# Four blocks of the first merge gate move from the stream to the opening, and the adaLN columns are turned by the identity

## The chip, the cores and the metric

The kernel runs on one core of a Trainium2 chip. The metric is device time in microseconds (us); the median of three runs before the change is 2131.4 us (2131.13 to 2132.64). The engines are named as the profile names them: PE is TensorE (PEld its weight loads), DVE is VectorE, ACT is ScalarE, POOL is GpSimd, SP is SyncE, which issues most DMAs.

## The reference

One layer of a decoder step with two parallel branches. The inputs are 256 prompt tokens and 8 samples of 8 tokens, so 320 token columns in all; the model width is 2048.

```python
mod = silu(c) @ w_ada + b_ada                       # 9 conditionings, 3 x 2048 features
shift, scale, gate = split(mod, 3)
h = rms_norm(x, pre_norm_g) * (1 + scale) + shift
(a_qkv, a_z, a_b, a_a, b_q, b_k, b_v, b_z, i_q, i_k, i_w, g_a, g_b) = split(h @ w_in)
y_a = gdn_branch(a_qkv, a_z, a_b, a_a, ...)         # gated delta rule, chunked
y_b = attend(b_q, b_k, b_v, i_q, i_w, i_k) * silu(b_z)
merged = sigmoid(g_a) * (y_a @ w_pa) + sigmoid(g_b) * (y_b @ w_pb)
out = rms_norm(merged @ w_out, post_norm_g)
return x + gate * out, ...
```

`attend` picks the top keys with an indexer (`i_q`, `i_k`, `i_w`) and attends to them only; for the samples the keys and values lie in a paged cache and are gathered. `g_a`, the input of the first merge gate, is 2048 features of `w_in`: 16 blocks of 128. Everything is float32 in and out.

## The kernel before, in words

**Products.** A block is 128 output features by 320 token columns, summed over 16 blocks of 128 input features. The weights are split into a high part (`whi`, a copy by ACT into the type that PE multiplies in one pass) and the remainder (`wlo`, a subtraction by DVE); the tokens `h` are split the same way into `xh` and `xl`. Each block of weights is used in three matmuls: `xh` by `whi`, `xl` by `whi`, `xh` by `wlo`. A block of the input projection is thus 16 x 3 = 48 matmuls.

**The opening** (`startup`, L493). The tokens `h` are not there at first: they need the conditioning `mod`, a product of `cT` (the nine conditionings, padded to 32 columns, stationary) with `w_ada`. The opening works in eight visits, q = 0 to 7. Visit q has these pieces:

- `columns`: the product of `cT` with the features of visit q, 256 of the shift and 256 of the scale, from four 1 MB loads. Four column groups of PE work side by side, each on every fourth block of input features, so that a bank of PSUM holds four partial sums in its four groups of 32 rows. ACT copies the bank to `msb`.
- `operands(q - 1)`, "the turn": six transposes of the tokens, then four float32 matmuls of `msb` with `sel`, which add the four partial sums and turn the features to the rows; DVE then makes `mod`, `gs`, `hT` and `xl`, ACT makes `xh`, for the two blocks of tokens of visit q - 1.
- `split_i(q - 1)` and `split(q - 1)`: high and low halves of the weights of the index queries (`whi`, `wlo`) and of a group of small projections (`awh`, `awl`; one buffer each).
- jobs, which queue in a first-in first-out list (`fifo`) and are taken by `run(n)`: per visit eight `iq_job` (index queries; 6 matmuls of 256 columns into a bank of PSUM, which two additions of DVE, into `q` and `qiS`, empty), one `bv_job`, and five `held_job` (6 matmuls of 320 columns each, into banks kept for the whole opening).

Three banks of PSUM go round among columns, turns and jobs. Each engine works its instructions off in the order in which this code writes them.

**The stream** (`stream`, L382) then takes one half block after the other (24 matmuls), from a list of chunks made in `attn_chunks` (the other index queries, queries, z, first gate, some more z) and `gdn_chunks`. Between them, generators ("sides") are stepped: the attention of the prompt, the eight samples (`sample_branch` and its successor), the gate of `mod` (`gate_gen`, which has columns and `sel` of its own kind), the delta rule. A planner decides when a side goes on, with a table of its own of how long instructions last. The first chunk of the delta rule may begin only when no side is left (`chunks[0].ready = lambda: not self.sides`, L1634): what the sides still have to do is then written out at once, with nothing of the stream in between.

One sample of the attention is, on PE, `esel` (the mask), `a,qS` (scores), 33 small `ident,a` (transposes of the probabilities), `a,a` and `vS,a` (products with the values), and one `ident,a` of 128 columns (the output); between these DVE takes maxima, ACT exponentials, DVE transposes the keys of the next sample (STREAM_TRANSPOSE), and POOL gathers keys and values.

Of the kernel before, what the change touches and what calls it, by code (L numbers as in the profile page):

```python
# [35 lines left out]
EARLY = 8  # L36
AHEAD = 4
# [167 lines left out]
class Kernel:  # L205
# [259 lines left out]
    def consts(self):  # L465
# [6 lines left out]
        self.ident_b = self.l0.tile([128, 128], BF, name="ident_b")  # L472
        v.tensor_copy(self.ident_b, self.ident)
# [19 lines left out]
    def startup(self):  # L493
# [12 lines left out]
        awl = sp.tile([128, 2, 720], F32R, name="awl")  # L506
        seq = []
        for q in range(8):
            seq += [("a", q, 0), ("a", q, 1), ("a", 8 + q, 0), ("a", 8 + q, 1), ("i", q, 0), ("w", q, 0)]
        raws, aws, iqs = {}, {}, {}  # L510
        pos = {"n": 0}

        def load():
            while pos["n"] < len(seq):
                kind, q, h = seq[pos["n"]]
                r = awr if kind == "w" else ring
# [8 lines left out]
                elif kind == "w":  # L525
                    for d0, c0, n in ((0, C_IK, 144), (144, C_BA, 64), (208, C_BK, 512)):
                        nc.sync.dma_start(t[:, :, d0:d0 + n], w[rows, c0:c0 + n].rearrange("(k p) c -> p k c", p=128))
                    aws[q] = t
                else:
# [15 lines left out]
        for e in range(2):  # L545
            nc.scalar.dma_start(x[2][64 * e:64 * e + 64], xs[:, 1024 * e:1024 * e + 1024])
# [21 lines left out]
        seli = sp.tile([128, 9, 4], I32, name="seli")  # L568
        nc.gpsimd.iota(seli, pattern=[[-1, 9], [-32, 4]], base=0, channel_multiplier=1)
        self4 = sp.tile([128, 9, 4], F32, name="self4")  # L570
        nc.vector.tensor_scalar(self4, seli, 0.0, None, op0=OP.is_equal)
        self.sel = self.l0.tile([128, 9], F32, name="sel")
        nc.vector.tensor_reduce(self.sel, self4, axis=AX.X, op=OP.add)
# [17 lines left out]
        both = sp.tile([128, 128], F32, name="both")  # L591
        for e in range(2):
            self.tt(both[:, 64 * e:64 * e + 64], self.ident[:, 0:64], self.ident[:, 64:128], OP.add)
# [23 lines left out]
        msb = sp.tile([128, 512], F32, name="msb")  # L617
# [14 lines left out]
        def split_i(q, g):  # L632
# [13 lines left out]
            low()  # L646

# [48 lines left out]

        def first_jobs():
# [8 lines left out]
        def jobs(q):  # L706
# [12 lines left out]
        def columns(q, e, h, p):  # L719
            t, whole = raws.pop((q + 8 * e, h))  # L720
            for k in range(8):
                kb, j = 8 * h + k, k % 4
                self.mm(p[32 * j:32 * j + 32, 256 * e:256 * e + 256], self.cT[:, kb, :], t[:, k, :], start=(kb < 4),
                        stop=(kb >= 12), skip=True)
            drop(t, whole)

        def operands(q, turned=None):
# [3 lines left out]
            for e in range(4):  # L731
                self.mm(p[:, 9 * e:9 * e + 9], msb[:, 128 * e:128 * e + 128], self.sel)
# [3 lines left out]
            for e, qq in enumerate((q, 8 + q)):  # L736
                self.tt(mod[:, 2 * qq:2 * qq + 2, :], p[:, 18 * e:18 * e + 18].rearrange("p (e s) -> p e s", s=9),
# [11 lines left out]
        for q in range(8):  # L749
# [12 lines left out]
            else:  # L762
                idle_turns(10)
# [6 lines left out]
            if q == 0:  # L770
                idle_turns(14)
            columns(q, 0, 1, p)
            if q == 0:
                idle_turns(14)
            elif q == 1:
                run(4)
            else:
                split(q - 1)
                run(5)
            if q >= AHEAD:  # L780
                split_i(q, 0)
            columns(q, 1, 0, p)
            if q == 0:
# [5 lines left out]
                idle_turns(8)  # L789
            columns(q, 1, 1, p)  # L790
            self.act(msb, p)
# [4 lines left out]
            elif q > 1:  # L796
                run(4)
# [10 lines left out]
        jobs(7)  # L808
        run(5)
        split(7)  # L810
        run(4)
        self.split_ahead(1)
        run(3)
        self.split_ahead(2)
        run(2)
# [12 lines left out]
    def gate_gen(self):  # L828
# [13 lines left out]
        for q in range(8):  # L842
# [6 lines left out]
            for k in range(KB):  # L849
                j = k % 4  # L850
                self.mm(p[32 * j:32 * j + 32, 0:256], self.cT[:, k, :], pend[k // 8][:, 256 * (k % 8):256 * (k % 8) + 256],
                        start=(k < 4), stop=(k >= 12), skip=True)
# [7 lines left out]
            self.act(m[:, 0:256], p[:, 0:256])  # L860
# [4 lines left out]
            for e in range(2):  # L865
                self.mm(p[:, 9 * e:9 * e + 9], m[:, 128 * e:128 * e + 128], self.sel)
            for e in range(2):
                k = 2 * q + e
                self.ts(self.gatp[:, k, :], p[:, 9 * e:9 * e + 9], self.feat[:, 32 + k:33 + k], self.feat[:, 64 + k:65 + k],
                        OP.add, OP.mult)  # L870
# [40 lines left out]
    def modulate(self, k, p, gs, mod, h):  # L911
        self.ts(h[:, :NP], p[:, :NP], gs[:, k, 0:1], mod[:, k, 0:1], OP.mult, OP.add)
        hs = h[:, NP:NT].rearrange("p (b t) -> p b t", t=TS)
        c0 = NP + 64 * (k // 8)
        bc = lambda a: a[:, k, 1:9].rearrange("p (b o) -> p b o", o=1).to_broadcast([128, NB, TS])
        self.tt(hs, p[:, c0:c0 + 64].rearrange("p (b t) -> p b t", t=TS), bc(gs), OP.mult)
# [86 lines left out]
    def attn_chunks(self):  # L1003
# [5 lines left out]
        ga = self.pairs(w, C_GA, 16, lambda p, h: self.gate_done(p, h, self.d_siga, self.t_r), r)  # L1009
# [1437 lines left out]
```

## Time and profile before

| | |
|---|---|
| median of three runs | 2131.4 us (2131.13 to 2132.64) |
| profiled execution, its own time | 2132.65 us |
| its span in the profile | 2130.9 us |
| PE busy | 2099.3 us, 99% |
| DVE, ACT, POOL busy | 1410.9, 989.6, 463.1 us |
| bytes moved by DMA | 438.91 MB, 206 GB/s on the mean |
| granted PE clock, mean | 0.998 |

The span is one execution as the profiler saw it; the times are those of executions without it. Busy time is an average over stages with different limits, so the stages are read one at a time: the opening lasts to about 170 us, the samples lie between 560 and 720 us. In a timeline a row gives start and length in us, engine, line, operation and tiles, how many instructions it holds, and in brackets the idle time before it with what ended it.

### The profile page before, as it was taken

The page shows a single profiled execution, that of the slowest core. Times are in us where ns is not written, and L with a number is a line of the kernel's source. Part 1 is how long each engine was busy: PE and PEld are TensorE (multiplying, and loading weights), DVE is VectorE, ACT ScalarE, POOL GpSimd, SP SyncE. Part 2 cuts the span into 40 slices and gives each one's busy share as a digit, 9 for nine tenths or more (in the row PEclk, how much of TensorE's full clock was granted, in tenths as well). Part 3 has the DMA queues.
Part 4 walks back from the last instruction along what each step waited for, and adds up shares of the span by engine and source line. Part 5 has one row for each costly group of instructions (what it writes and reads, how often), then busy time and mean ns, then how long its engine had stood idle before and what let it go on. Part 6 is the DMA issues. An engine that isn't in the chain of part 4 may idle for free.

```text
span 2130.9 us, 43963 instructions
## 1 busy us (share of the span) xinstructions
PE 2099.3 (99%) x17055; PEld 2006.3 (94%) x17055; DVE 1410.9 (66%) x2881; ACT 989.6 (46%) x2257; POOL 463.1 (22%) x653
## 2 busy tenths in 40 slices
PE   7999999999999999999999999999999999999997
PEld 5889999899999999999999999999999999999997
DVE  4665657899755678868787878787746545445543
ACT  3235464333344455565656565656535424233343
POOL 2000100000001036545444444445440000000000
PEclk9999999999999999999999999999999999999999
DMA  9996656985787766777877777777787967555562
GB/s 332 355 309 173 181 151 178 289 256 151 201 238 239 205 181 173 211 210 207 207 200 199 208 196 210 193 212 192 200 218 210 268 180 218 161 155 146 166 178 85
DMA packets 720336, 438.91 MB, mean 206 GB/s; under 512 B 74144, under 2 KB 705536, under 8 KB 717824
## 3 DMA queue, kind: packets, MB, share of 16 engines
q1 hardware_dynamic: 716032, 413.45, 68.9%
q0 software_dynamic: 3616, 21.02, 3.0%
q8 instruction: 134, 2.20, 0.4%
q10 hardware_dynamic: 480, 1.65, 0.3%
q14 instruction: 74, 0.61, 0.1%
HBM read 386.81 MB, written 48.94 MB: 204 GB/s over the span
## 4 chain that ended last, share of the span: by engine, by line
PE 72%; issue 23%; DMA 2%; DVE 2%; ACT 0%; SPq 0%; DVEq 0%; POOL 0%; POOLq 0%; ACTq 0%
PE pm L63 56%; PE ps L63 16%; DMA raw<-in_w_ada_dram 1%; DVE S L63 1%; DMA rawx<-in_w_in_dram 1%; DVE wlo L63 0%; SPq L63 0%; DMA c<-in_c_sample_dram 0%; DVE awl L63 0%; DMA out_dram<-S 0%; ACT whi L63 0%; ACT ot L63 0%; DVE sga L63 0%; DVE w L63 0%; DVEq L2443 0%
## 5 line engine op out<-in xcount | busy, mean ns | idle before, releaser
L63 PE MATMUL pm<-xh,whi 128*128 128x320 f32 (+1 forms) x3284 | 996.1, 317 | 1.9 <-DVE qiS L63 0.8
L63 PE MATMUL pm<-xl,whi 128*128 128x320 f32 (+1 forms) x3284 | 962.1, 307 | 0.4 <-DVE xl L63 0.3
L63 DVE TENSOR_TENSOR wlo<-raw,whi 128x1024 fp32r<-128x1024 f32 x474 | 589.1, 1252 | 280.8 <-ACT whi L63 264.9
L63 PEld LDWEIGHTS pm<-xh,whi 128*128 128x128 f32 x3284 | 617.6, 188 | 32.2 <-issue 23.9
L63 PEld LDWEIGHTS pm<-xl,whi 128*128 128x128 f32 x3284 | 618.1, 188 | 1.7 <-DVE xl L63 0.8
L63 ACT ACTIVATE whi<-raw 128x1024 fp32r<-128x1024 f32 x474 | 497.7, 1058 | 169.7 <-PE pm L63 150.8
L63 PE MATMUL pm<-xh,wlo 128*128 128x320 f32 (+1 forms) x3284 | 547.6, 307 | 0.0
L63 PEld LDWEIGHTS pm<-xh,wlo 128*128 128x128 f32 x3284 | 495.4, 188 | 0.0
L63 POOL TENSOR_TENSOR X<-X,tmpx 48x31 f32<-48x31 f32 (+15 forms) x248 | 175.9, 709 | 19.4
L63 POOL TENSOR_TENSOR tmpx<-blk,X 48x31 f32<-48x31 f32 (+15 forms) x248 | 160.4, 647 | 51.0 <-DMA blk<-d_b 32.8
L63 PE MATMUL pm<-y1h,whi 128*128 128x320 f32 x512 | 151.3, 308 | 1.1 <-ACT y1h L63 1.1
L63 PE MATMUL pm<-y1l,whi 128*128 128x320 f32 x512 | 151.3, 307 | 0.2
L63 DVE SCALAR_TENSOR_TENSOR ps<-xp,cs,ps 128x344 f32<-128x344 f32 x192 | 111.5, 581 | 6.8
L63 POOL TENSOR_TENSOR rfin<-rfin,mh 128x3 f32<-128x3 f32 x1 | 0.8, 848 | 486.4 <-DVE rfin L63 486.4
L63 POOL TENSOR_TENSOR sc<-sc,mh 128x6 f32<-128x6 f32 (+1 forms) x24 | 43.6, 1815 | 277.0 <-DVE sc L63 213.0
L63 PEld LDWEIGHTS pm<-y1h,whi 128*128 128x128 f32 x512 | 95.7, 187 | 1.4 <-ACT y1h L63 1.3
L63 PEld LDWEIGHTS pm<-y1l,whi 128*128 128x128 f32 x512 | 96.1, 188 | 0.7 <-DVE y1l L63 0.7
L63 PE MATMUL pm<-y1h,wlo 128*128 128x320 f32 x512 | 85.4, 308 | 0.0
L63 PEld LDWEIGHTS pm<-y1h,wlo 128*128 128x128 f32 x512 | 77.7, 187 | 0.0
L63 DVE SCALAR_TENSOR_TENSOR S<-S,gtr,ps 128x128 f32<-128x128 f32 x256 | 67.4, 341 | 0.1
L63 ACT ACTIVATE xp<-pm 128x256 f32<-128x256 f32 (+1 forms) x128 | 32.0, 304 | 69.9 <-PE pm L63 69.9
L63 ACT ACTIVATE ot<-ot,sc 128x128 f32<-128x128 f32 x96 | 29.9, 390 | 72.3 <-DVE sc L63 72.3
(374 smaller groups left out, 2308.0 us busy)
## 6 DMA issues: line engine op xcount, KB each, us to landing
raw<-in_w_in_dram SPq DMA_DIRECT2D x336, 512.0 KB
raw<-in_w_pa_dram SPq DMA_DIRECT2D x64, 512.0 KB
rawx<-in_w_ada_dram SPq DMA_DIRECT2D x18, 1024.0 KB
a<-in_w_ada_dram SPq DMA_DIRECT2D x16, 1024.0 KB
S<-in_state_gdn_dram SPq DMA_DIRECT2D x32, 512.0 KB
out_dram<-S SPq DMA_DIRECT2D x32, 512.0 KB
raw<-in_w_pb_dram SPq DMA_DIRECT2D x32, 512.0 KB
raw<-in_w_out_dram SPq DMA_DIRECT2D x32, 512.0 KB
```

The source lines that it names most:

```text
L63: made = fn(*args, **kw)
```

## The change

Four of the 16 blocks of the first gate are computed in the opening. A new buffer `gwr` takes 0.5 MB per visit for them, `split_g` makes their halves, four `ga_job` per visit stand in the list behind `bv_job`, and their sums go to SBUF by additions of DVE; after the last visit come tanh, the affine step and the store. The chunk list of the stream has 12 blocks of the first gate instead of 16.

The columns are computed in two calls instead of four per visit. Each call takes the tile of the shift and the one of the scale, and each column group of PE sums one block of 128 features over all inputs. There are no partial sums to add, and `msb`, now 128 columns, is turned by one transpose with the identity. The gate's generator does the same. The sample tokens come in one DMA, with the two halves of the features in alternating rows.

The order in a visit is another: `split(q - 1)` and three jobs stand before the first call of `columns`.

```diff
+GATED = 4
         for q in range(8):
-            seq += [("a", q, 0), ("a", q, 1), ("a", 8 + q, 0), ("a", 8 + q, 1), ("i", q, 0), ("w", q, 0)]
+            seq += [("a", q, 0), ("a", 8 + q, 0), ("a", q, 1), ("a", 8 + q, 1), ("i", q, 0), ("w", q, 0), ("g", q, 0)]
...
+        def split_g(q):
+            r = gws.pop(q)
...
+            self.act(hv[:, :, :128 * GATED], r)
+            self.tt(lv[:, :, :128 * GATED], r, hv[:, :, :128 * GATED], OP.subtract)
+            gwr.put(r)
+            load()
...
+        def ga_job(q, j):
+            hi, lo, hv, lv = halves[q, 2]
+            p = self.ps_main.get()
+            products(q, p[:, :NT], hv, lv, 128 * j, 128, True, True)
+            add_to(q, p, [(ga[j], p[:, :NT])])
...
+            for j in range(GATED):
+                fifo.append(lambda j=j: ga_job(q, j))
...
-        def columns(q, e, h, p):
-            t, whole = raws.pop((q + 8 * e, h))
+        def columns(q, h, p):
+            pair = [raws.pop((q + 8 * e, h)) for e in range(2)]
             for k in range(8):
-                kb, j = 8 * h + k, k % 4
-                self.mm(p[32 * j:32 * j + 32, 256 * e:256 * e + 256], self.cT[:, kb, :], t[:, k, :], start=(kb < 4),
-                        stop=(kb >= 12), skip=True)
+                kb = 8 * h + k
+                for j in range(4):
+                    f = 128 * (j % 2)
+                    self.mm(p[32 * j:32 * j + 32, 0:128], self.cT[:, kb, :], pair[j // 2][0][:, k, f:f + 128],
+                            start=(kb == 0), stop=(kb == KB - 1), skip=True)
...
-            for e in range(4):
-                self.mm(p[:, 9 * e:9 * e + 9], msb[:, 128 * e:128 * e + 128], self.sel)
+            self.tr(p[:, 0:128], msb)
...
             if q == 1:
                 run(2)
                 split(0)
-                run(2)
+                run(3)
+            elif q > 1:
+                split(q - 1)
+                run(3)
             p = self.ps_main.get()
-            columns(q, 0, 0, p)
...
-            columns(q, 0, 1, p)
...
-                split(q - 1)
-                run(5)
+            columns(q, 0, p)
...
+                    run(3)
+                    split_g(q - 1)
+                    run(2)
             if q >= AHEAD:
                 split_i(q, 0)
-            columns(q, 1, 0, p)
...
-            columns(q, 1, 1, p)
-            self.act(msb, p)
+            columns(q, 1, p)
+            self.act(msb, p[:, 0:128])
...
-            elif q > 1:
-                run(4)
+            else:
+                run(3 if q == 1 else 5)
...
         run(5)
         jobs(7)
+        split(7)
         run(5)
-        split(7)
+        split_g(7)
         run(4)
...
-        ga = self.pairs(w, C_GA, 16, lambda p, h: self.gate_done(p, h, self.d_siga, self.t_r), r)
+        ga = self.pairs(w, C_GA + 128 * GATED, 16 - GATED,
+                        lambda p, h: self.gate_done(p, GATED + h, self.d_siga, self.t_r), r)
```

The first place is a visit of the opening, q = 3, on PE: the end of the held jobs and what follows. In these rows `awh` and `awl` belong to the held jobs, `whi` and `wlo` to the index queries, `cT` to the columns; the number behind a name is its buffer. Before:

```order
L63 MATMUL ps_71<-xl,awh 128x320
L63 MATMUL ps_71<-xh,awl 128x320 x2
L63 MATMUL ps_72<-raw_75,cT 32x256 x8
L63 MATMUL ps_72<-raw_76,cT 32x256 x8
L63 MATMUL pm_66<-xh,whi_79 128x256
...
L63 MATMUL pm_66<-xh,wlo_82 128x256 x2
L63 MATMUL pm_65<-xh,whi_79 128x256
```

With the change:

```order
L64 MATMUL ps_71<-xh,awl 128x320 x2
L64 MATMUL pm_65<-xh,whi_78 128x256
...
L64 MATMUL pm_65<-xh,wlo_81 128x256 x2
L64 MATMUL ps_72<-xh,whi_78 128x256
...
L64 MATMUL ps_72<-xh,wlo_81 128x256 x2
L64 MATMUL pm_66<-xh,whi_78 128x256
...
L64 MATMUL pm_66<-xh,wlo_81 128x256 x2
L64 MATMUL pm_65<-raw_75,cT 32x128 x2
L64 MATMUL pm_65<-raw_76,cT 32x128 x2
```

The columns stood right behind the held jobs, in a bank of their own; now three index-query jobs stand between, and the columns go into the bank of the first of these, `pm_65`. On DVE the same place now reads:

```order
L64 TENSOR_TENSOR wlo_82<-rawx_162,whi_79 128x1024
L64 TENSOR_TENSOR awl<-awr_165,awh 128x1440
L64 TENSOR_TENSOR q_139<-ps_72,q_139 128x192
L64 TENSOR_TENSOR qiS<-ps_72,qiS 128x8x8
L64 TENSOR_TENSOR q_140<-pm_65,q_140 128x192
L64 TENSOR_TENSOR qiS<-pm_65,qiS 128x8x8
```

`awl` stands ahead of the additions that empty the banks of the index-query jobs, as it did before.

The second place is the samples at the end of the attention, on PE. Before, sample 7, the last, from the end of its scores to its products with the values, cut to one row of each kind:

```order
L63 MATMUL ps_72<-a_1771,qS 64x256 x2
L63 MATMUL pm_66<-xh,whi_79 128x320
...
L63 MATMUL ps_67<-ident,a_1772 128x128
...
L63 MATMUL pm_65<-xh,wlo_83 128x320 x8
L63 MATMUL ps_71<-ident,a_1773 128x32
...
L63 MATMUL ps_72<-ident,a_1773 64x128
L63 MATMUL pm_65<-xh,whi_78 128x320
...
L63 MATMUL pm_65<-xh,wlo_81 128x320 x8
L63 MATMUL ps_71<-a_1769,a_1772 64x128 x16
L63 MATMUL ps_71<-vS,a_1772 64x128 x2
```

With the change, from the last stream matmul ahead of sample 5 to the beginning of sample 6:

```order
L64 MATMUL pm_65<-xh,wlo_81 128x320 x8
L64 LDWEIGHTS esel
...
L64 MATMUL ps_70<-a_2258,qS 64x256 x2
L64 MATMUL ps_67<-ident,a_2260 128x128
L64 MATMUL ps_72<-ident,a_2261 128x32
...
L64 MATMUL ps_70<-ident,a_2261 64x128
L64 MATMUL ps_67<-a_2259,a_2260 64x128 x16
L64 MATMUL ps_67<-vS,a_2260 64x128 x2
L64 LDWEIGHTS esel
L64 MATMUL ps_72<-bs,esel 128x256
```

The stream's matmuls (`whi`, `wlo`) that lay between the parts of a sample are not there in samples 5, 6 and 7; the first one comes after the last row of sample 7.

More of the change, by code (lines that the diff above doesn't have):

```diff
@@ L506, in startup @@
         awl = sp.tile([128, 2, 720], F32R, name="awl")
+        gwr = Ring([sp.tile([128, 2, 128 * GATED], F32, name="gwr")])
+        ga = [self.auxf[:, 0:NT], self.vtok.rearrange("p c d -> p (c d)")[:, 0:NT]]
+        ga += [sp.tile([128, NT], F32, name=f"ga{j}") for j in range(GATED - 2)]
         seq = []
         for q in range(8):
-            seq += [("a", q, 0), ("a", q, 1), ("a", 8 + q, 0), ("a", 8 + q, 1), ("i", q, 0), ("w", q, 0)]
-        raws, aws, iqs = {}, {}, {}
+            seq += [("a", q, 0), ("a", 8 + q, 0), ("a", q, 1), ("a", 8 + q, 1), ("i", q, 0), ("w", q, 0), ("g", q, 0)]
+        raws, aws, iqs, gws = {}, {}, {}, {}
         pos = {"n": 0}
@@ L515, in load @@
                 kind, q, h = seq[pos["n"]]
-                r = awr if kind == "w" else ring
+                r = {"w": awr, "g": gwr}.get(kind, ring)
                 if not r.free:
@@ L528, in load @@
                     aws[q] = t
+                elif kind == "g":
+                    nc.sync.dma_start(t, w[rows, C_GA:C_GA + 128 * GATED].rearrange("(k p) c -> p k c", p=128))
+                    gws[q] = t
                 else:
@@ L544, in startup @@
         xs = i["x_sample"].rearrange("b t d -> (b t) d")
-        for e in range(2):
-            nc.scalar.dma_start(x[2][64 * e:64 * e + 64], xs[:, 1024 * e:1024 * e + 1024])
+        nc.scalar.dma_start(x[2], xs.rearrange("r (e c) -> (r e) c", e=2))
         nc.scalar.dma_start(x[1], i["x_prompt"][0, 128:256, :])
@@ L616, in startup @@
         gs = sp.tile([128, KB, 9], F32, name="gs")
-        msb = sp.tile([128, 512], F32, name="msb")
+        msb = sp.tile([128, 128], F32, name="msb")
         hT = [sp.tile([128, NT], F32, name=f"hT{j}") for j in range(2)]
@@ L646, in split_i @@
             low()
+        def split_g(q):
+            r = gws.pop(q)
+            hi, lo = self.whi.get(), self.wlo.get()
+            hv, lv = (x.rearrange("p k c -> p (k c)").rearrange("p (k c) -> p k c", k=2) for x in (hi, lo))
+            halves[q, 2] = hi, lo, hv, lv
+            self.act(hv[:, :, :128 * GATED], r)
+            self.tt(lv[:, :, :128 * GATED], r, hv[:, :, :128 * GATED], OP.subtract)
+            gwr.put(r)
+            load()
         def upper(q, a, hi, c0, n, start, t0=0):
@@ L695, in iq_job @@
                 del halves[q, h // 4]
+        def ga_job(q, j):
[3 more added lines that the diff above has]
+            add_to(q, p, [(ga[j], p[:, :NT])])
+            if j == GATED - 1:
+                self.whi.put(hi)
+                self.wlo.put(lo)
+                del halves[q, 2]
+            if q == 7:
+                t = ga[j]
+                self.act(t, t, AF.Tanh, scale=0.5)
+                self.ts(t, t, 0.5, 0.5, OP.mult, OP.add)
+                nc.sync.dma_start(self.d_siga[j], t)
         def first_jobs():
@@ L848, in gate_gen @@
             p = self.psum()
[L849 to L852, printed above, removed]
+            for k in range(8):
+                for j in range(4):
+                    kb = 2 * k + j // 2
+                    c0 = 256 * (kb % 8) + 128 * (j % 2)
+                    self.mm(p[32 * j:32 * j + 32, 0:128], self.cT[:, kb, :], pend[kb // 8][:, c0:c0 + 128],
+                            start=(k == 0), stop=(k == 7), skip=True)
             while pend:
@@ L864, in gate_gen @@
             p = self.psum()
-            for e in range(2):
-                self.mm(p[:, 9 * e:9 * e + 9], m[:, 128 * e:128 * e + 128], self.sel)
+            self.tr(p[:, 0:128], m[:, 0:128])
             for e in range(2):
                 k = 2 * q + e
-                self.ts(self.gatp[:, k, :], p[:, 9 * e:9 * e + 9], self.feat[:, 32 + k:33 + k], self.feat[:, 64 + k:65 + k],
-                        OP.add, OP.mult)
+                self.ts(self.gatp[:, k, :], p[:, 32 * e:32 * e + 9], self.feat[:, 32 + k:33 + k], None, OP.add)
+                self.tt(self.gatp[:, k, :], p[:, 64 + 32 * e:73 + 32 * e], self.gatp[:, k, :], OP.add)
+                self.ts(self.gatp[:, k, :], self.gatp[:, k, :], self.feat[:, 64 + k:65 + k], None, OP.mult)
             self.ps_side.put(p)
```

46 lines of the change are left out of this document (19 added, 27 removed).

## The prediction

> **What bounds the kernel now.** I began with the page, then read the opening (0 to 170 us) in windows and in the chain of waits, and the attention phase in the timelines.
>
> ```profile
> span 2130.9 us, 43963 instructions
> ...
> PE 2099.3 (99%) x17055; PEld 2006.3 (94%) x17055; DVE 1410.9 (66%) x2881; ACT 989.6 (46%) x2257; POOL 463.1 (22%) x653
> ...
> PE 72%; issue 23%; DMA 2%; DVE 2%; ACT 0%; SPq 0%; DVEq 0%; POOL 0%; POOLq 0%; ACTq 0%
> ```
>
> TensorE (PE) is busy 99% of the span, and of the chain that ends last it holds 72% itself and its own issue most of the rest. So work that leaves PE's queue is worth its duration, work that moves within it is worth nothing, and what makes PE stand still costs its full length. The windows of the opening and of the samples (columns: length, then busy time and count of PE, PEld, DVE, ACT, POOL, the granted clock, DMA share, GB/s):
>
> ```profile
> 20.00:40.00 20.00, 17.48 (x167) 13.38 (x164) 8.26 (x22) 6.75 (x13) 0.00 (x0) 1.00 1.09 354
> 40.00:60.00 20.00, 17.80 (x180) 13.42 (x179) 9.81 (x26) 5.50 (x8) 0.00 (x0) 1.00 1.08 362
> 60.00:80.00 20.00, 19.74 (x183) 17.05 (x184) 12.22 (x36) 5.33 (x7) 0.00 (x0) 1.00 1.08 353
> 80.00:100.00 20.00, 18.90 (x172) 15.80 (x172) 12.90 (x35) 5.68 (x7) 0.00 (x0) 1.00 1.08 354
> ...
> 160.00:180.00 20.00, 18.82 (x144) 18.29 (x143) 11.82 (x28) 8.91 (x24) 5.02 (x6) 1.00 0.70 201
> 560.00:720.00 160.00, 159.53 (x1887) 146.13 (x1886) 88.99 (x170) 64.46 (x157) 16.57 (x27) 1.00 0.77 227
> ```
>
> PE is idle 2.5 + 2.2 + 0.3 + 1.1 + 1.2 = 7.3 us in the opening (in the windows left out, 100 to 160, it never is), and 0.5 us in the whole stretch of the samples. The granted clock is full.
>
> **The products of the moved blocks.** The chain shows the held jobs of two visits, and one index-query job:
>
> ```profile
> 118.42 4.45 PE ps L63 x30
> ...
> 152.79 4.45 PE ps L63 x30
> 157.25 0.72 PE pm L63 x6
> ```
>
> 30 matmuls of 320 columns take 4.45 us, 148 ns each; the two rows lie two visits apart, so a visit lasts 17.2 us. Four gate blocks are 4 x 48 = 192 such matmuls: 28.4 us more in the opening (24 matmuls, 3.55 us, in each of eight rounds) and 28.4 us less in the stream. These cancel. Their additions are DVE's, which is busy 12 to 13 us of a 20 us window; four more of about 0.5 us and one low half of 1.2 us a visit fit.
>
> **The turn.** The timeline of PE in the visit that begins at 99.47, and the group of the same turn in the second gate:
>
> ```profile
> 99.47 0.82 PE L63 MATMUL pm<-ident,x 128*128 128x128 f32 x6
> 100.22 1.06 PE L63 MATMUL ps<-sel,msb 128*128 128x9 f32 x8
> 101.13 0.35 PE L63 MATMUL ps<-xh,awh 128*80 128x320 f32 x1
> ...
> 105.65 1.93 PE L63 MATMUL ps<-rawx,cT 128*32 128x256 f32 x32
> 107.52 0.39 PE L63 MATMUL pm<-xh,whi 128*128 128x256 f32 x1
> ```
>
> ```profile
> L63 PE MATMUL ps<-sel,s 128*128 128x9 f32 x32 | 4.0, 236 | 0.0
> ```
>
> Eight `sel` instructions hold PE for 0.91 us (100.22 to 101.13); one transpose by the identity, of the kind of the six before them (0.75 us), holds it 0.12. That saves 0.79 us in each of eight visits, 6.3 us. In the stream, four `sel` instructions (0.114 us each at the same rate) become one transpose in each of eight turns: 8 x (0.46 - 0.12) = 2.7 us. Together 9.0. The narrow copy of `msb`, 128 for 512 columns, shortens ACT only, which is not waited for here.
>
> The column products keep their volume: 16 matmuls of 256 columns (32 instructions, 1.87 us, 105.65 to 107.52) become 32 of 128, four feature groups side by side as now. At an equal rate per column that is 1.87 us again; at 30 ns an instruction (the `a,qS` row below: 64 in 1.92 us) it is 1.92. Far bound: an instruction keeps its present 58 ns, 1.87 us more in each of 24 calls (16 here, 8 in the second gate), 45 us. I take zero, since the `a,qS` row, also of small tiles side by side, lies at the near end.
>
> **The new order in a visit.** After the held jobs PE now runs three index-query jobs and only then the columns. What those jobs wait for stands in the chain of the visit that begins at 63.85, and, without the second `wlo`, in the timeline of DVE two visits later:
>
> ```profile
> 63.85 4.78 PE ps L63 x34
> ...
> 71.01 1.57 DVE awl L63
> 72.58 0.27 DVE q L63
> 72.85 0.14 DVE qiS L63
> ```
>
> ```profile
> 106.95 1.66 DVE L63 TENSOR_TENSOR awl<-awr,awh 128x1440 fp32r<-128x1440 f32 x1 [0.64 <-ACT awh L63]
> ...
> 108.81 0.21 DVE L63 TENSOR_TENSOR qiS<-pm,qiS 128x64 f32<-128x64 f32 x1
> ```
>
> The additions that free a job's bank stand behind `awl` on DVE, and `awl` cannot be rewritten before the held jobs (ending at 68.63, and ahead of 105.65) have read the old one. The first bank comes free 4.36 us after the held jobs in visits 2 to 4 (72.99 less 68.63), 3.4 us after them in later ones (109.02 less 105.65). Before, PE filled that time with the columns (1.87 us) and two jobs. Now it does three jobs, 2.15 us, and the columns, which take the first job's bank, wait: 2.2 us in visits 2, 3 and 4, 1.2 us in 5, 6, 7 and at the end. That is 11.4. Behind the columns PE's whole queue waits.
>
> Of the old idle, the largest stop is a transfer:
>
> ```profile
> 52.86 0.85 PE L63 MATMUL pm<-raw,cT 128*32 128x256 f32 x12 [1.84 <-DMA raw<-in_w_ada_dram]
> ```
>
> The 2.5 us of the window from 20 I keep, the other 4.8 I let go, since each visit gives its loads about 3.8 us more. So the waits change by 11.4 - 4.8 = +6.6. Lower bound: no bank is waited for and all the old idle is filled, -7.3. Upper bound: all the old idle stays, +11.4.
>
> Opening in all: 28.4 - 6.3 + 6.6 = **+28.7**. As to transfers, a visit loads 0.5 MB more, 1.5 us at 354 GB/s against 3.8 us of longer visit, so they stay hidden. The single buffer of the new loads can hold back those behind it on SP's queue; if each of six visits lost what that late transfer and its like cost in the window from 40 (2.2 us), it would be 13.
>
> **The samples lose their cover.** With four gate blocks fewer, the stream reaches the first block that has to wait for all samples eight half blocks earlier. In the new order samples 5, 6 and 7 stand on PE with no stream matmul between their parts; before, only the last step of sample 7 did. One sample, in the timelines of PE, then DVE, then ACT and the DMA issues:
>
> ```profile
> 680.90 0.31 PE L63 MATMUL ps<-bs,esel 32*128 32x256 bf16 x5
> 681.13 1.98 PE L63 MATMUL ps<-a,qS 32*64 32x256 f32 x64
> 683.05 0.42 PE L63 MATMUL pm<-xh,whi 128*128 128x320 f32 x1
> ...
> 688.63 0.92 PE L63 MATMUL ps<-ident,a 32*128 32x32 f32 x33
> ...
> 696.52 1.97 PE L63 MATMUL ps<-a,a 128*64 128x128 f32 x32
> 698.42 0.44 PE L63 MATMUL ps<-vS,a 64*64 64x128 f32 x4
> ...
> 700.75 0.31 PE L63 MATMUL ps<-bs,esel 32*128 32x256 bf16 x5
> ...
> 715.65 0.33 PE L63 MATMUL ps<-ident,a 128*128 128x128 f32 x1 [0.47 <-ACT a L63]
> ```
>
> ```profile
> 683.12 1.42 DVE L63 TENSOR_REDUCE st<-ps 128x1 f32<-128x256 f32 x4 [1.10 <-PE ps L63]
> ...
> 687.23 0.16 DVE L63 RECIPROCAL st<-st 128x1 f32<-128x1 f32 x1
> ...
> 688.19 2.37 DVE L63 STREAM_TRANSPOSE a<-a 128x1024 f32<-128x1024 f32 x2
> ...
> 691.58 0.28 DVE L63 TENSOR_TENSOR ybuf<-ps,ybuf 128x128 f32<-128x128 f32 x1
> 691.78 0.93 DVE L63 COPY a<-ps 128x256 f32<-128x256 f32 x3
> ```
>
> ```profile
> 686.78 0.22 ACT L63 ACTIVATION_READ_ACCUMULATOR a<-ps,st 128x1 f32 x1
> ```
>
> ```profile
> a<-in_cache_v_dram,idx POOLq DMA_INDIRECT x1, 7.6
> ```
>
> A covered sample takes 19.85 us (680.90 to 700.75) with 96 stream matmuls in it, so it costs PE 19.85 - 96 x 0.148 = 5.65. Bare, its parts follow each other: scores to +2.2, maxima and exponentials to +6.1 (687.00), the reciprocal to +6.5 (687.39), then in DVE's queue the next sample's keys, 2.37, to +8.9, `ybuf` 0.3 and the copies 0.9 to +10.1, and the products with the values 2.2: +12.3. The values' gather, 7.6 us from an issue behind the scores, lands at about +10 too. Idle: 6.65 us in samples 5 and 6; sample 7 has no next keys, 4.2; of that 0.5 stood there already (715.65). Sum **+16.9**. Lower bound, with the keys in no chain: 3 x 4.2 - 0.5 = 12. Upper bound, two gathers in series in samples 5 and 6 (15.2 us): 2 x 9.55 + 6.5 - 0.5 = 25.
>
> **Sum.** Opening +28.7, stream -28.4 - 2.7, samples +16.9: **+14.5**. The profiled execution took 2132.65 us (the span and 1.75 around it), so 2147.2 on its own ground. It lies 1.25 above the median of 2131.4, from which I get **2146**.
>
> **Rivals.** (1) The other side: the moved jobs fill the opening. They need no operand of their own visit; if their 3.55 us cover the old 7.3 us of idle and no bank is waited for, opening and turns give -7.3 - 9.0 = -16.3, against 12 to 16.9 for the samples: 2127 to 2132. It can be told from no change once the bare samples cost under 12. For it: DVE is free 7 us of 20. Against: the moved jobs stand behind the index queries in PE's queue, not where the wait is.
>
> (2) Bare samples meet the clock. PE idles in one from +2.2 to +6.1 and from +7.0 to +10.1; the longest stop in the rows of before is the 1.84 us at 52.86, and the clock of that window is full. If it halved, the 5.3 us of PE work in a bare sample (2.2, 0.9 and 2.2) could take twice as long: 3 x 5.3 = 16 on top, 2162. [...]
>
> (3) Loads held back on SP's queue (+13) or columns paid by the instruction (+45): 2159 to 2191. Against: DMA's rate leaves 2 us a visit, and the `a,qS` row shows 30 ns.
>
> **How the numbers follow.** Chances: forecast 0.70, (1) 0.14, (2) 0.09, (3) 0.07. The forecast's own range is 2134 to 2155: samples 12 to 25 and some 6 us of waits either way. For 8 in 10 I reach down into (1) and up towards (2): 2130 to 2159. A measurement of this kernel tells about 0.2% (4.3 us) from no change. Faster: half of (1), 0.07. Same: the rest of (1) and 0.04 of the forecast's lower end, 0.11. Slower: 0.82.
>
> **What would show it.** Opening: held jobs 21 us apart instead of 17.2, PE waiting for DVE `qiS` ahead of the columns, the stream beginning some 29 us later. Turn: one identity transpose of 0.12 us. Samples: the last three 12.3, 12.3 and 10 us long with PE idle half of it, released by DVE and ACT. The forecast is wrong if the last samples are covered after all, if the columns begin without a wait, or if the granted clock falls below 1 in the samples.

## The result

The changed kernel takes 2155.57 us (median of four runs, 2154.58 to 2156.99) against 2131.8 us before: 23.8 us more, a ratio of 1.0111 with a 95% interval of 1.0097 to 1.0125. The forecast was 2146, 14.5 us more. The direction was right; the size was short by 9 us.

The profiled execution of the changed kernel took 2156.99 us. Its page, and its windows (columns as in the prediction: length, busy time and count of PE, PEld, DVE, ACT, POOL, the granted clock, DMA share, GB/s):

```profile
span 2155.2 us, 45401 instructions
...
PE 2099.4 (97%) x17745; PEld 2024.0 (94%) x17745; DVE 1424.2 (66%) x2938; ACT 989.2 (46%) x2261; POOL 464.2 (22%) x652
```

```profile
20.00:200.00 180.00, 166.82 (x1943) 156.78 (x1943) 113.55 (x287) 55.04 (x82) 8.67 (x8) 1.00 0.92 295
400.00:480.00 80.00, 76.16 (x871) 72.38 (x871) 71.23 (x144) 24.01 (x50) 2.58 (x2) 1.00 0.97 286
480.00:500.00 20.00, 20.00 (x153) 19.49 (x154) 14.31 (x27) 6.23 (x8) 0.94 (x1) 0.93 0.75 233
700.00:740.00 40.00, 24.38 (x418) 18.51 (x417) 15.01 (x44) 10.26 (x40) 3.34 (x9) 0.74 0.35 118
```

PE is busy 2099 us, as before, although some 9 us of work were taken from it: what it has left runs partly at a lower clock (0.93 from 480 to 500, 0.74 from 700 to 740), and the two cancel. Its idle time has grown from 31.6 to 55.8 us, which is as much as the span has grown (24.3 us). The growth lies in three places: 13.2 us of idle time in the opening (7.3 before), 3.8 us between 400 and 480 (none before) and 15.6 of 40 us from 700 on (0.5 before). What PE waited for, from 20 to 1800 us:

```profile
PE ps L64 <- ACT a L64: 12.0, 5, 3.8
PE pm L64 <- DVE qiS L64: 6.2, 6, 1.3
PE ps L64 <- DVE qiS L64: 4.2, 4, 1.4
PE ps L64 <- issue: 4.1, 2, 2.3
PE ps L64 <- DMA a<-in_w_ada_dram: 3.8, 2, 2.7
```

The columns of these rows are total, number and longest wait. The first and the fourth are the samples, the second and third are mostly the columns of the opening behind DVE's additions (9.6 of the 10.4 us), and the last, which no step of the forecast has, is the second gate in the stream, waiting for its weights.

A visit of the opening on PE and DVE: the turn, then the end of the third index-query job, the columns, and what DVE does meanwhile.

```profile
89.57 0.82 PE L64 MATMUL pm<-ident,x 128*128 128x128 f32 x6
90.31 0.33 PE L64 MATMUL ps<-ident,msb 128*128 128x128 f32 x1
90.39 0.39 PE L64 MATMUL ps<-xh,awh 128*80 128x320 f32 x1
...
97.28 0.40 PE L64 MATMUL pm<-xh,wlo 128*128 128x256 f32 x2
98.84 0.30 PE L64 MATMUL ps<-rawx,cT 128*32 128x128 f32 x2 [1.16 <-DVE qiS L64]
...
100.72 0.39 PE L64 MATMUL pm<-xh,whi 128*128 128x256 f32 x1
```

```profile
96.73 1.65 DVE L64 TENSOR_TENSOR awl<-awr,awh 128x1440 fp32r<-128x1440 f32 x1
98.30 0.35 DVE L64 TENSOR_TENSOR q<-ps,q 128x192 f32<-128x192 f32 x1
98.57 0.22 DVE L64 TENSOR_TENSOR qiS<-ps,qiS 128x64 f32<-128x64 f32 x1
```

One transpose (90.31) stands where eight `sel` instructions stood. The columns begin at 98.84, right after the addition that ends at 98.79, and their 64 instructions take 1.88 us (98.84 to 100.72). The held jobs of neighbouring visits lie 21.1 to 21.6 us apart. The last held job ends at 196.7 us, at 169.5 before: the opening is 27.2 us longer.

The last three samples on PE:

```profile
700.04 0.31 PE L64 MATMUL ps<-bs,esel 32*128 32x256 bf16 x5
700.28 1.98 PE L64 MATMUL ps<-a,qS 32*64 32x256 f32 x64
...
706.19 1.42 PE L64 MATMUL ps<-ident,a 32*128 32x32 f32 x33 [3.67 <-ACT a L64]
709.41 4.02 PE L64 MATMUL ps<-a,a 128*64 128x128 f32 x32 [1.79 <-issue]
713.36 0.69 PE L64 MATMUL ps<-vS,a 64*64 64x128 f32 x4
713.98 0.44 PE L64 MATMUL ps<-bs,esel 32*128 32x256 bf16 x5
...
723.89 4.02 PE L64 MATMUL ps<-a,a 128*64 128x128 f32 x32 [2.29 <-issue]
...
728.47 0.41 PE L64 MATMUL ps<-bs,esel 32*128 32x256 bf16 x5
...
736.07 3.53 PE L64 MATMUL ps<-a,a 128*64 128x128 f32 x32 [0.32 <-ACT a L64]
...
740.48 0.33 PE L64 MATMUL ps<-ident,a 128*128 128x128 f32 x1 [0.52 <-ACT a L64]
```

They last 13.9, 14.5 and 12.0 us, with no stream matmul in them. The pauses are where the forecast put them: 3.67 to 3.77 us behind the scores, 1.8 and 2.3 us ahead of the products in samples 5 and 6. But the products with the values, `a,a`, take 3.95 us to the next start (709.41 to 713.36) where they took 1.90 before. The same windows cut at the changes of the clock say why:

```profile
701.40:704.80 3.40, 1.12 (x33) 0.52 (x17) 2.01 (x8) 0.89 (x5) 0.94 (x1) 1.00 0.95 303
704.90:715.00 10.10, 7.01 (x90) 5.54 (x98) 4.02 (x10) 2.27 (x9) 0.94 (x1) 0.50 0.30 109
...
718.50:721.90 3.40, 0.92 (x33) 0.69 (x33) 1.21 (x4) 2.57 (x12) 0.05 (x2) 1.00 0.93 308
722.00:728.60 6.60, 4.71 (x40) 3.98 (x41) 2.31 (x5) 0.11 (x1) 0.00 (x0) 0.50 0.02 6
732.10:735.50 3.40, 0.71 (x33) 0.67 (x33) 0.85 (x5) 2.23 (x10) 0.00 (x0) 1.00 0.01 2
735.60:738.90 3.30, 2.98 (x27) 2.77 (x28) 0.89 (x3) 0.63 (x2) 0.00 (x0) 0.50 0.00 0
```

The rows at 701.40, 718.50 and 732.10 are stretches of 3.4 us in which PE was busy for 1.12, 0.92 and 0.71 us; behind each of them the granted clock is 0.50.

### The profile page after: what moved, and what is told of

The parts are those of the page before. It is cut to its first block, busy times and chain, and to the rows that moved or that the text cites. A ratio compares the mean times of both kernels' runs of the same rounds, so it can differ in the third digit from the quotient of the medians.

```text
span 2155.2 us, 45401 instructions
## 1 busy us (share of the span) xinstructions
PE 2099.4 (97%) x17745; PEld 2024.0 (94%) x17745; DVE 1424.2 (66%) x2938; ACT 989.2 (46%) x2261; POOL 464.2 (22%) x652
## 4 chain that ended last, share of the span: by engine, by line
PE 42%; issue 23%; DVE 1%; ACT 1%; DMA 0%; DVEq 0%; POOL 0%; POOLq 0%; SPq 0%; ACTq 0%
PE pm L64 33%; PE ps L64 8%; DVE S L64 1%; ACT a L64 0%; DMA out_dram<-S 0%; ACT ot L64 0%; DVE wlo L64 0%; DVE st L64 0%; DVE sga L64 0%; DVE w L64 0%; DVEq L2475 0%; ACT whi L64 0%; DVE ps L64 0%; POOL sc L64 0%; DVE sc L64 0%
## 5 line engine op out<-in xcount | busy, mean ns | idle before, releaser
L64 DVE TENSOR_TENSOR wlo<-raw,whi 128x1024 fp32r<-128x1024 f32 x466 | 582.4, 1260 | 242.7 <-ACT whi L64 231.8
L64 ACT ACTIVATE whi<-raw 128x1024 fp32r<-128x1024 f32 x466 | 488.5, 1057 | 178.7 <-PE pm L64 161.4
```

Of the source, the lines that this page charges most:

```text
L64: made = fn(*args, **kw)
```

## The experiments

Twelve kernels ran. Differences are of medians against the kernel before in the same batch (2132.1 to 2133.5 us); the changed kernel stands at +23.8.

**Columns first.** The changed kernel, the columns put right behind the held jobs again.

```diff
-            elif q > 1:
-                split(q - 1)
-                run(3)
             p = self.ps_main.get()
             columns(q, 0, p)
...
-                    run(3)
+                    split(q - 1)
+                    run(6)
                     split_g(q - 1)
```

> The changed kernel (2155.6 us) with one part undone: in visits 2 to 7 the first call of the columns stands right behind the held jobs again, the three index-query jobs behind it. In the trace of the changed kernel PE stands 1.1 to 1.4 us for DVE's qiS ahead of the columns in each of these visits, 7.7 us in six. Theory (the new order makes that wait): it goes, but a smaller one comes back at the third job (bank free 3.4 to 4.4 us after the held jobs, columns and two jobs fill 3.3), so 3 to 7 us less, 2149 to 2152.5, and visits under 20.6 us apart. Rival (DVE is the limit of the visit, the wait only moves): within 2 us of the changed kernel. The samples and the second gate stay as in the changed kernel on both theories.

Measured: 2151.21 us, +18.8 (ratio 1.0088, 1.0071 to 1.0105), so 5.0 less than the change. Its waits from 20 us to the end of the opening:

```profile
PE ps L64 <- DVE qiS L64: 1.8, 2, 1.4
PE pm L64 <- DVE qiS L64: 1.6, 2, 1.3
```

10.4 us of waits for `qiS` became 3.4, and the last held job ends at 192.2 instead of 196.7. The theory holds: the new order made that wait. The early visits now wait 1.8 us more for loads and for `xh` (3.4 us against 1.6), which is most of the rest.

**The turn alone.** No gate blocks in the opening (`gwr`, `split_g` and `ga_job` are gone), the old order of a visit, but the new columns and the identity in the opening and in the second gate.

```diff
-GATED = 4
+GATED = 0
...
-            elif q > 1:
-                split(q - 1)
-                run(3)
             p = self.ps_main.get()
             columns(q, 0, p)
...
+                    split(q - 1)
+                    run(5)
             if q >= AHEAD:
```

> The turn alone: columns in the new form (128 wide, four feature groups) and the identity transposes, in the opening and in the second gate; no gate block in the opening, the old order of a visit, 16 gate blocks in the stream. Theory: 9.0 us less PE work; in its order of instructions the second gate's turns stand some 60 matmuls later than before and sample 7 alone is bare, which costs 4 us of idle time and 1 to 2 of clock. So 3 to 5 us faster than before, 2126.5 to 2129. Rival (the short column products cost more than the old ones, or the loads in pairs make PE wait): no gain or slower, 2131 to 2140, to be seen as columns over 1.95 us for 64 instructions or as waits for the w_ada loads in the opening.

Measured: 2139.42 us, +7.0 (1.0033, 1.0021 to 1.0046). The theory was wrong, and the time lies in the rival's range: a change that takes 9 us of work from PE makes the kernel slower. Sample 7 is bare as expected, but the opening (granted clock 0.91 from 20 to 60 us) and the second gate (2.0 us idle between 400 and 480) also wait for loads. Two later runs take this apart.

**Cover for the samples.** The changed kernel with four more z blocks taken ahead of the delta rule.

```diff
-EARLY_Z = (0, 4)
+EARLY_Z = (0, 2, 4, 6)
```

> The changed kernel with four more z blocks taken ahead of the delta rule (EARLY_Z of four pairs instead of two), so that the stream again has matmuls between the parts of samples 5, 6 and 7 (96 between any two). No work is added. Theory (bare samples cost their idle time and slow the clock): the 15.6 us of PE idle time there and the 7 us of slow matmuls go, 2131 to 2135; granted clock 1.00 from 700 to 770 us; the late loads of the second gate (3.8 us) stay. Rival (the samples only show a delay that comes back elsewhere, for example because the delta rule's first group then lacks the z blocks as cover): 2143 or more, with PE idle time after 770 us that the changed kernel does not have.

Measured: 2175.55 us, +43.1 (1.0198, 1.0181 to 1.0215): the rival. Windows and waits (the latter from 740 to 1000 us):

```profile
700.00:740.00 40.00, 40.00 (x494) 36.63 (x486) 22.09 (x43) 17.97 (x43) 3.33 (x9) 1.00 0.77 231
...
800.00:900.00 100.00, 82.96 (x664) 80.01 (x666) 66.66 (x150) 42.45 (x114) 51.32 (x78) 0.88 0.63 159
```

```profile
PE ps L64 <- DMA X<-d_x: 15.1, 2, 12.6
```

From 700 to 740 PE is full and its clock 1.00, so samples 5 and 6 are cured by matmuls between their parts. Sample 7, which begins at 738.97, is bare again (4.5 us idle and a clock of 0.91 from 740 to 760). And 17 us of idle time now lie between 800 and 900, where the changed kernel has none: the delta rule's first steps wait for a transfer (`X` from `d_x`) for which the changed kernel does not wait. By this reading the z blocks had covered it. Stream matmuls are cover, and there is only one stock of them.

**Filled samples, twice.** The changed kernel with 30 and 20 transposes of the identity in the two pauses of samples 5, 6 and 7; nothing reads what they write. First into a PSUM bank of the samples that seemed free:

```diff
+            if b >= 5:
+                d = [t for t in self.ps_side.free if all(t is not u for u in ps)][0]
+                for _ in range(30):
+                    nc.tensor.transpose(d[:, 0:128], self.ident, self.ident)
             self.a8.put(K.pop(b))
...
+            if b >= 5:
+                d = [t for t in self.ps_side.free if all(t is not u for u in ps + [p])][0]
+                for _ in range(20):
+                    nc.tensor.transpose(d[:, 0:128], self.ident, self.ident)
             yield self.ready(pT, V[b])
```

> The changed kernel with idle transposes of the identity (50 of 109 ns in each of samples 5, 6 and 7) put into PE's pauses, in a bank that nobody reads; samples stay bare and the chain of DVE and ACT is not shortened. Theory (PE's pauses of 3.7 us lower its clock, and that is why the products with the values take 4.0 us instead of 1.9): granted clock 1.00 in the samples, products back to 1.9 to 2.0 us, samples 12.3, 12.3 and 10 us long instead of 13.9, 14.5 and 12.1, in all 5 to 8 us less, 2148 to 2151. Rival (the products are slow for another reason, such as the gathers into the same buffers or the memory banks): the products stay at 3.5 to 4 us and the time within 1.5 us of the changed kernel.

Measured: 2160.12 us, +27.7 (1.0125, 1.0108 to 1.0142), slower than the change. The fill itself waited:

```profile
708.07 4.53 PE L64 MATMUL ps<-ident 128*128 128x128 f32 x20 [1.92 <-DVE ybuf L64]
712.53 2.73 PE L64 MATMUL ps<-a,a 128*64 128x128 f32 x32
...
740.19 2.35 PE L64 MATMUL ps<-ident 128*128 128x128 f32 x20
742.47 1.97 PE L64 MATMUL ps<-a,a 128*64 128x128 f32 x32
```

In sample 5 the bank still had to be read by `ybuf`, the transposes began 1.92 us late, ran at half clock (0.50 from 710 to 714; 4.5 us for 20, 2.35 in sample 7) and held up the products. In sample 7 (740.19) nothing waited, and the products took 1.90 us. So this run said something on the mechanism, but not on the price. The second time the transposes went into a bank of the stream's accumulators (`self.ps_main.free[0]` for `d`):

> The changed kernel with idle transposes in PE's pauses of samples 5, 6 and 7 once more, now in a bank of the stream's accumulators that nothing reads or writes there (in the run before, the bank was still to be read by ybuf, and the transposes waited for it). Theory (pauses lower the clock): granted clock 1.00 from 700 to 740 us, products with the values 1.9 to 2.0 us in all three samples, samples 12.5, 12.5 and 10 us, 2147 to 2151. Rival (the fill cannot keep the clock, or delays the chain as much as it gains): 2154 to 2158.

Measured: 2151.0 us, +18.9 (1.0089, 1.0072 to 1.0106), 4.9 less than the change, by adding 150 useless transposes.

```profile
700.00:740.00 40.00, 37.19 (x536) 32.91 (x535) 19.31 (x46) 11.78 (x41) 7.08 (x17) 1.00 0.39 132
```

The clock is 1.00 throughout. The products take 2.24, 2.24 and 1.90 us, and the three samples together take 36.9 us instead of 40.4; these 3.6 us are the gain of the fill. The rest lies before the samples, where the fill does nothing: in this trace the opening and the second gate wait 1.7 us less, and the clock behind the second gate's wait stayed at 1.00. In sample 5 the products begin 3.2 us behind the start of the transposes of the probabilities in both kernels, so the chain of DVE and ACT is the same: the clock is the cause of the slow products.

**The old form of the second gate.** The changed kernel with `gate_gen` as it was before (`sel`, 256 wide columns).

```diff
-            for k in range(8):
-                for j in range(4):
-                    kb = 2 * k + j // 2
...
+            for k in range(KB):
+                j = k % 4
+                self.mm(p[32 * j:32 * j + 32, 0:256], self.cT[:, k, :], pend[k // 8][:, 256 * (k % 8):256 * (k % 8) + 256],
+                        start=(k < 4), stop=(k >= 12), skip=True)
```

> The changed kernel with one part undone: the second gate's generator in the stream has its old form again (256 wide columns in four partial sums, turned by sel); the opening is that of the changed kernel. In the order of its instructions the samples now begin 60 matmuls of the stream earlier, so sample 5 keeps 60 of its 96 matmuls and samples 6 and 7 stay bare. Theory (the new form of the gate, through the planner's pacing, took one more sample's cover and brought the late w_ada loads): the 3.8 us of waits for a<-in_w_ada_dram and about 1.5 us of slow clock behind them go, the idle time in the samples falls by 4 to 7 us, its slow matmuls by 2, and 2.7 us of sel come back: 2143 to 2149. Rival (both come from the moved gate blocks alone): waits and samples as in the changed kernel, 2155 to 2159.

Measured: 2145.48 us, +13.4 (1.0065, 1.0048 to 1.0082), 10.4 less than the change.

```profile
400.00:480.00 80.00, 80.00 (x684) 72.65 (x683) 68.70 (x119) 26.24 (x51) 0.94 (x1) 1.00 0.97 289
...
700.00:740.00 40.00, 29.90 (x393) 25.59 (x392) 17.03 (x42) 11.96 (x37) 6.50 (x16) 0.83 0.50 163
```

The idle time between 400 and 480 is gone, and that from 700 to 740 falls from 15.6 to 10.1. In the order of its instructions the samples begin 60 stream matmuls earlier, behind 1764 of them as in the kernel before, where the changed kernel has 1824; sample 5 has 60 of its 96 matmuls back. So the rest of the third bare sample was not due to the moved blocks but to the gate's new form, to which the planner gave another pace. Why that form's loads come late is not shown; every run with it has 1.8 to 3.8 us of idle time between 400 and 480, none with the old form has any.

**The turn in the opening only.** The kernel with the turn alone, and the old gate.

> The kernel before with the turn by the identity in the opening only (old gate in the stream, no gate blocks in the opening, old order of a visit). The samples stand in the order as before, all covered. Theory (the opening without the moved blocks is near the rate of its transfers, 354 GB/s, so that PE time saved there turns into waits for w_ada loads, and those slow the clock): of 6.3 us saved, 2 to 4 arrive, 2128 to 2131 against 2132 before. Rival A (the saving arrives whole): 2126. Rival B (the run with the turn alone, 7 us slower than before, lost its time in the opening): 2135 or more.

Measured: 2129.93 us, -2.2 (0.9989, 0.9979 to 0.9998). The interval lies below 1, though the gain is smaller than the 0.2% named in the prediction. The windows, the cause of the loss, and the same stretch of the kernel before:

```profile
20.00:60.00 40.00, 34.52 (x462) 30.62 (x464) 17.83 (x46) 11.48 (x21) 0.00 (x0) 0.91 1.08 358
60.00:140.00 80.00, 78.19 (x1031) 72.11 (x1020) 52.96 (x148) 22.40 (x30) 0.00 (x0) 1.00 1.08 355
```

```profile
51.20 3.06 PE L64 MATMUL pm<-raw,cT 128*32 128x128 f32 x60 [2.37 <-DMA raw<-in_w_ada_dram]
```

```profile
60.00:140.00 80.00, 78.64 (x718) 67.61 (x718) 52.15 (x147) 22.90 (x30) 0.00 (x0) 1.00 1.08 355
```

DMA runs at 355 GB/s and a share of 1.08 to 140 us in both. The PE time saved meets the transfers: a stop of 2.37 us for a load, with the clock lowered (0.91 over the window). The last held job ends at 167.0, 2.5 us earlier than before; 6.3 were taken away. This run differs from the turn alone only in the gate, so the gate's new form costs 9.2 us there too (+7.0 against -2.2).

**Both undone.** The changed kernel with the columns first and the old gate.

> The changed kernel with two parts undone: columns right behind the held jobs, and the old form of the second gate. Theory: the two gains add up, 4 to 5 us of the first and 7 to 12 of the second: 2139 to 2145; what is left over before (2132) is then the bare samples 6 and 7 and their clock, less the sel saved in the opening. Rival (both only make the same wait shorter): not below 2146.

Measured: 2141.44 us, +9.3 (1.0044, 1.003 to 1.0059). The gains add up (5.0 and 10.4 make 15.4, 14.5 measured). The last held job ends at 192.1; less the 28.4 of moved work that is 163.7, 5.8 us before the old end. With the moved blocks in it the opening is held less by its transfers (323 GB/s between 60 and 140 us instead of 355, and 3.0 us of waits for its loads from 20 us on instead of 4.4), and by this sum nearly all of the saved turn arrives there.

**Two blocks.** The changed kernel, and then the one with both parts undone, with two gate blocks in the opening.

```diff
-GATED = 4
+GATED = 2
```

> The changed kernel with two gate blocks in the opening instead of four (GATED = 2), all else as in the change. In its order of instructions sample 5 has its 96 stream matmuls back, samples 6 and 7 are bare. Theory (the time grows by the bare samples, not by the blocks moved): one bare sample less, 6.65 us of idle time and about 2 of slow matmuls: 2145 to 2149; the second gate's waits for its loads stay; the opening's waits ahead of the columns stay too. Rival (the cost goes with the work put into the opening): 2143 or less, half of the way between the turn alone (2139) and four blocks (2156) or below it, with the gain in the opening and not in the samples.

> Two gate blocks in the opening, columns right behind the held jobs, and the old form of the second gate: what the runs so far found harmful is undone, as far as it goes with moved blocks. In its order sample 6 keeps 60 of 96 stream matmuls and sample 7 is bare. Theory: the turn saves up to 6.3 us in an opening that the moved blocks hold off the rate of its transfers, one bare sample and a part of another cost 6 to 9: 2130 to 2137, 4 to 10 us under the same kernel with four blocks (2141). Rival (the bare samples are only a small part of the loss): 2139 to 2143.

Measured: 2160.64 (+28.3; 1.0134, 1.0117 to 1.0151) and 2143.57 (+11.3; 1.0052, 1.0035 to 1.0068), the first slower than with four blocks (+23.8), the second not clearly (+9.3). Both theories failed. The samples did what was expected (in both, one sample's 96 matmuls are back), the opening did not. The first kernel's waits from 20 us on:

```profile
PE pm L64 <- DVE qiS L64: 10.1, 8, 2.4
PE pm L64 <- ACT whi L64: 3.5, 3, 1.2
PE pm L64 <- DVE wlo L64: 1.6, 3, 0.5
```

The number of jobs taken per visit had stayed at 18 where a visit now brings 16, so jobs ran ahead of the halves that they need. That was a second change in my edit, not a size alone. With the numbers put right:

```diff
                     split_g(0)
-                    run(3)
+                    run(2)
...
                     split_g(q - 1)
-                    run(2)
+                    run(1)
...
-                run(3 if q == 1 else 5)
+                run(2 if q == 1 else 4)
```

> The changed kernel with two gate blocks in the opening, as in the run of two blocks before it, but with the numbers of jobs taken at each place of a visit lowered from 18 to the 16 that a visit now has. (With 18 taken, jobs ran a little ahead of the halves and additions that they need, and PE stood 9 us longer in the opening.) Theory (bare samples): the opening's waits are those of the change, one bare sample less: 2145 to 2149. Rival (fewer moved blocks make the opening itself wait longer, since its transfers run at their rate): 2152 or more, with PE waiting for loads in the opening.

> The same numbers of jobs for the kernel with two moved blocks, the columns right behind the held jobs and the old form of the second gate. Theory: against the same kernel with four blocks (2141.4) one bare sample less, 6 to 8 us, against 2 us more of waits for loads in the opening: 2133 to 2138, still not below the kernel before (2132), since sample 7 and part of sample 6 are bare. Rival: 2140 or more, if the opening loses with its transfers what the samples gain.

Measured: 2147.01 (+13.5; 1.0067, 1.005 to 1.0084) and 2133.73 (+0.3; 0.9999, 0.9989 to 1.0008). Both as the theory had it: with two blocks fewer moved, one bare sample less, they stand 10.3 and 9.0 us below the same kernels with four blocks. No kernel with moved blocks is faster than the one before; only the turn in the opening alone is, by 0.1%.

Step by step from the kernel before, the loss reads: turn in the opening -2.2, four blocks moved +11.5 (to +9.3), the new order of a visit +4.1 (to +13.4), the new form of the second gate +10.4 (to +23.8). The sizes depend on the order of the steps: the gate's new form costs 9.2 without the moved blocks, and the new order of a visit 5.0 when the gate has its new form.

## Why the prediction was right, and where it fell short

**What bounds the kernel: right, but two rules drawn from it were too strong.** Every part of the loss is PE standing still or PE slowed down. But "work that leaves PE's queue is worth its duration" failed in the opening without moved blocks, where 6.3 us left and 2.2 arrived, and "work that moves within it is worth nothing" failed for the stream, where moving four blocks cost 11.5 us.

**The size, place by place.** Opening: +0.3 forecast (28.7 less the 28.4 moved), -1.2 measured (27.2 less 28.4). Samples: +16.9 forecast; samples 5 to 7 last 40.4 us, where the forecast counts 3 x 5.65 us of work, so +23.5, or +23.0 without the half microsecond of idle time that stood there before. Second gate: -2.7 forecast; 3.8 us of waits and about 1.5 us of half clock behind them (an estimate: half of the 2.94 us that PE is busy from 479.5 to 482.9 us, where the granted clock is 0.51), less the 2.7, make +2.6. So the samples' term was 6.1 us short and the gate's 5.3, and 1.5 us of the opening hid a part. The time lies just above the forecast's own range (2134 to 2155), in the part of the wider one (2130 to 2159) that was kept for rival (2).

**Products and turn: right.** The moved products cancel. The turn's one transpose takes about 0.1 us, and the short columns cost what the long ones did, 1.88 us for 64 instructions against 1.87. One reading was wrong, without weight: the kernel before does wait once for ACT's copy of `msb`, 0.65 us at 97.31 us.

**The order in a visit: right.** The forecast had waits of 2.2 and 1.2 us, 11.4 in all, in visits 2 to 7 and at the end; measured there are 8.2 us, 1.0 to 1.3 each (6.9 of them in the six visits, not the 7.7 that the first experiment's expectation says). Another 1.4 us ahead of the columns of visit 1 was not in the forecast. In visits 2 to 4 the forecast was nearly twice too high: in the visit shown the first bank came free 3.9 us after the held jobs (98.79 less 94.88) instead of 4.4, and the three jobs, of which the first also waits for `wlo`, filled 2.8 us of it instead of 2.15. Idle time in the opening is 13.2 us, against 7.3 + 6.6 = 13.9. "The other 4.8 I let go" nearly holds for the change, and the runs show its condition: with the moved blocks the transfers run at 310 GB/s between 60 and 140 us, without them at 355, and there the same turn ran into the loads.

**The samples: right about the idle time, wrong about the clock.** The pauses came at the places of the forecast, the first with its length (3.7 us for 3.9), the second shorter (1.8 and 2.3 for 3.1); idle time grew by 15.6 us, against 16.9. What the term left out is the clock, which fell to 0.50 once in each of the three samples (704.9 to 715.0, 722.0 to 728.6 and 735.6 to 738.9). By the prediction's own sign this step was wrong: it named a granted clock below 1 in the samples, and the clock is 0.74 from 700 to 740. The forecast gave this to a rival of its own (0.09) and priced it at 16 us, all work at half clock. No row of the prediction shows the half in that price; in the trace of before the clock is 0.50 only from 2121 us on, behind PE's last matmul, while the changed kernel's samples show 0.50 in the three stretches named. It happened in part: the slow products alone (twice 2.05 and once 1.56) make 5.7 us, and filling the pauses won 3.6 in the samples. This belonged into the term, because the pauses that it computed, 3.9 and 3.1 us, were already far longer than the 1.84 us that it names as the longest stop in its rows of before.

**"With four gate blocks fewer": wrong as the whole cause.** That samples 5, 6 and 7 are bare the forecast read from the order of the instructions, rightly; the cause it gave covers two of them. Four blocks are 192 matmuls, two samples of 96. In the kernel before, sample 7 already has 60 instead of 96, and the gate's new form takes another 60: 192 + 36 + 60 are the 288 of three samples.

**The second gate: this step failed.** The forecast booked it as a pure gain, -2.7 us, four `sel` instructions for one transpose. Measured, undoing the new form gives 10.4 us back, a part of which the forecast had priced among the samples: the planner paces it otherwise, so that the samples begin 60 matmuls later and lose most of a sample's cover, and two of its loads come late (3.8 us, and the clock 0.93 in the window behind them). PE's cost of the operations was right; what a generator's new instructions do to a planner that times everything behind them was not looked at. In the order of the instructions it could be seen, by counting the stream's matmuls ahead of the first sample in both kernels (1764 and 1824).

## What to carry to other kernels

Work in a stream that keeps a busy engine fed is also the cover for chains that run beside it: before moving a block out of it, count what lies between the parts of each such chain in the new order, and price a chain without cover by its own length and by the clock that its pauses cost (here 0.74 from 700 to 740). A saving on the busiest engine arrives only where nothing else, here the transfers at 355 GB/s, is just behind it. When a planner orders the work, cost a new form by what it moves behind it as well as by its instructions, and change the numbers that pace the jobs together with the number of jobs.

## What the runs showed of the hardware

In the trace of the changed kernel the granted clock is 0.50 in four stretches between the opening and the end, 3.4, 10.2, 6.8 and 3.4 us long. These lengths and the distances between their starts (225.3, 17.1 and 13.7 us) are whole multiples of 3.41 us, so I cut the trace into steps of that length, counted from the start of the first. From 20 us on there are five steps at full clock in which PE was busy for 1.3 us or less, and each was followed by one at 0.50: 1.15 us from 476.1, 1.12, 0.92 and 0.71 in the rows above, 1.30 from 2141.8. In every other step at full clock PE was busy for 1.8 us or more (the least from 22.2 and from 715.1), and the clock stayed full behind it.

The length of a stop alone does not tell in these runs whether half clock follows. In the turn alone a stop of 1.96 us lies between 400 and 480, where the clock is 0.98; in the turn in the opening only there are stops of 2.0 and 2.37 us for loads, and the clock is 0.50 from 24.6 to 27.8 and from 51.9 to 55.1. But in the second filled run a stop of 2.8 us for the second gate's weights left the clock at 1.00 (400 to 500), and in two blocks with both parts undone one of 2.5 us did (20 to 60). The 2.8 us lay across two stretches in which PE was still busy for 1.70 of 3.4 us (from 474.0) and 2.31 of 3.3 (from 477.5). The stop of 1.84 us in the kernel before left the clock full too (1.00 from 40 to 60).

That filler work which nobody reads can pay was new to me: with 150 transposes in their pauses the three bare samples took 3.6 us less.
